# Seven half-block products for part of the output projection, a third buffer of low weight parts, and changed orders in a hybrid mLSTM / gated-MLP layer

## The chip, the core and the metric

The kernel runs on one core of a Trainium2 chip. Its engines have queues of their own: TensorE (PE, matmuls; PEld is its weight load), VectorE (DVE), ScalarE (ACT), GpSimd (POOL) and SyncE (SP), which here only issues DMAs. The metric is the device time of one execution in microseconds, the median of several runs.

## What is computed

One decoder layer over 512 tokens of width 2048: RMSNorm, one input projection (2048 to 14352 columns), two groups of heads, one output projection, residual, RMSNorm. In the reference, cut to what matters:

```python
xn = _rmsnorm(h, norm_w)
proj = jnp.einsum('bsd,de->bse', xn, w_in).astype(f32)
q, k, v_m, o_m, z_m, i_pre, f_pre, u_g, v_g, z_g = _split_cols(proj)
...
hm = _mlstm_chunkwise(q, k, v, log_i, log_f)          # 8 heads, after a causal convolution on q, k
y_m = rmsnorm(hm) * sigmoid(o_m) * silu(z_m)
...
y_g = gelu(u_g) * (W_s @ layernorm(gelu(v_g)) + b_s) * silu(z_g)
...
y = jnp.concatenate([y_m, y_g], axis=-1)
h = h + jnp.einsum('bse,ed->bsd', y, w_out)           # w_out: 4096 x 2048
return _rmsnorm(h, final_norm_w)
```

## The kernel before

All matmuls are in fp32r. For precision each operand is split into a high part (an fp32r copy, made by ACT) and a low part (the remainder, a subtraction on DVE), and each product is three matmuls: high x high, high x low, low x high.

**Stage 0** (L681 to 716) computes the first unit of the input projection in the plain way: eight steps j of 24 matmuls of 512 columns, with the gates' matmuls `gp` behind each. Beside it `split_x` and `sums_x` prepare the seven sums of blocks of x, `stats` the sums of squares, and `token_rows` (at j = 7) the row scales `r_b` with matmuls `rb_ps` from `diag` (DVE). The unit's results leave PSUM through eight Gelu activations (L713), which need `r_tok`.

**The input projection** (L719 to 748): 27 further units of 512 columns, each eight chunks of weights. A product of 2 x 2 blocks is made of seven products of sums of blocks (`PRODUCTS`, L32) in place of eight: 7 x 2 x 3 = 42 matmuls of 256 columns per chunk (L741). The seven results of a unit fill seven of the eight PSUM banks: the first four products the pool `pp`, the other three the pool `pm`, whose fourth bank serves background work. `combine` (L347) then forms the four result blocks: an ACT copy (L351) and seven DVE operations (L352 to 358). A bank is free for the next unit's product when the operation that reads it last is through; for q5 that is L356.

**Weights.** `load(n)` brings chunk n into `wf` (four buffers), four chunks ahead; a "str" chunk is five blocks of 256 columns by SP, after which POOL's DMA adds two blocks onto two others (L151). `split(n)`, two chunks ahead, forms two more sums in `we` on DVE (L175, L176), casts all seven to `wh` on ACT (L178, three buffers), and subtracts into `wl` on DVE (L179, two buffers). A "std" chunk of 1024 columns (L168, L169) serves stage 0 and the output projection.

**Background work** waits in `bg`, a queue of small steps; `run_bg(k)` runs k of them after each chunk: the activations, spatial mixing, transposes and convolution of the unit before, and in the output stage the heads of the mLSTM.

**The output projection** (L761 to 799): for the g half four column quarters dq of eight chunks, then for the mLSTM half ("m") four quarters of six chunks, all plain: 24 matmuls of 512 columns per chunk (L785 to 787), four accumulators in `pp`. While the g half runs, `gates`, `gate_columns` and the eight heads run as background, five steps a chunk: loads by POOL's queue, four score steps `st_s`, four value steps `st_sv`, `st_norm`, `st_out` (L618), and two transposes `turn` (L453) of the result `oz`, which is written to DRAM. In the last g quarter `load_y("m", g)` brings it back and splits it. The sums of the g half go through `acc_dram`.

**The last stage** (L812 to 844) adds the chunks g = 6, 7, plain, token tile by token tile, normalises and writes out.

Short-lived tiles come from a pool `tp` of 14 (tag "t"). The framework's planner, not the program text, sets the order in each engine's queue: it takes what its own model of time says is ready, earlier code first. On each engine the order is then fixed.

Of the kernel before, what the change touches and what calls it, by code (L numbers as in the profile page):

```python
# [32 lines left out]
    ("q1", 0, 1), ("q6", 4, 5), ("q2", 1, 0), ("q5", 6, 3), ("q7", 3, 4), ("q4", 2, 6), ("q3", 5, 2),  # L33
# [3 lines left out]
GAP_X, GAP_W = 32, 112  # L37
# [10 lines left out]
def hybrid_layer(ctx, tc, xs, x, w_first, w_mid, w_gate, w_out, par, bif, ws_t, sgu, fin_w, out):  # L48
# [7 lines left out]
    tp = pool("tp", 14)  # L56
# [9 lines left out]
    def temp(name, dt=F32):  # L66
        return tp.tile([P, S + 8], dt, tag="t", name=name)
# [85 lines left out]
    def split(n):  # L153
# [5 lines left out]
        if kind == "std":  # L159
# [3 lines left out]
            else:  # L163
                h, l = (wp.tile([P, WS], F32R, tag=tag, name=f"{tag}{n}", bufs=bufs)[
                    :, OFF:OFF + 1024].rearrange("p (a b) -> p a b", a=2) for tag, bufs in (("wh", 3), ("wl", 2)))
# [7 lines left out]
        l = wp.tile([P, WS], F32R, tag="wl", name=f"wl{n}", bufs=2)  # L173
        e = wp.tile([P, 2 * H], F32, tag="we", name=f"we{n}", bufs=2)
# [10 lines left out]
    def load_x(j):  # L185
        if j >= NP:
            return
        xr[j] = []
        for b in range(2):
            t = half(f"xr{j}_{b}")  # L190
# [5 lines left out]
    def split_x(j):  # L196
# [4 lines left out]
        a21 = tp.tile([P, S + 8], F32R, tag="t", name=f"a21_{j}")[:, 0:S].rearrange("p (a b) -> p a b", a=2)  # L201
# [27 lines left out]
    ssq16 = sm.tile([P, NT, 4], F32, tag="ssq16", name="ssq16", bufs=1)  # L229

    def stats(tt, half_):
        for c in (2 * half_, 2 * half_ + 1):
            t = temp(f"xt{tt}_{c}")[:, 0:S]
            nc.sync.dma_start(t, x[tt * P:(tt + 1) * P, c * S:(c + 1) * S])
            nc.scalar.activation(t, t, AF.Square, accum_out=ssq16[:, tt, c:c + 1])

    def stats_end():
        ssq = sm.tile([P, NT], F32, tag="s4", name="ssq", bufs=8)
        nc.vector.reduce_sum(ssq, ssq16, axis=mybir.AxisListType.X)
# [35 lines left out]
    def gate_spill():  # L275
        t = temp("gsp")[:, 0:S]
        nc.vector.tensor_tensor(t[0:GR, :], gp[0:GR, :], r_b[0:GR, :], op=ALU.mult)
        nc.gpsimd.dma_start(g_dram[0:GR, :], t[0:GR, :])
# [6 lines left out]
    def gates():  # L285
# [6 lines left out]
        for a, g in enumerate((li, xf)):  # L292
            nc.vector.scalar_tensor_tensor(g, in0=raw[2 + a], scalar=bif_t[:, a:a + 1], in1=g,
                                           op0=ALU.add, op1=ALU.add)
# [30 lines left out]
    def gate_columns():  # L325
        li, m, offs = gate_rows
        tps = pm.tile([P, 14, NH], F32, tag="m", name="tps")
        go = row("go")
        nn = 0
        for s0 in range(NT):  # L330
            for t0 in range(s0, NT):
# [6 lines left out]
                nc.tensor.transpose(tps[:, pair(s0, t0), :], src, ident[0:NH, 0:NH])  # L338
# [8 lines left out]
    def combine(un, q):  # L347
# [5 lines left out]
        v.tensor_tensor(a, a, ps["q2"], op=ALU.add)  # L353
        v.tensor_tensor(c, ps["q5"], b, op=ALU.subtract)
        v.tensor_tensor(d, b, ps["q7"], op=ALU.add)
# [8 lines left out]
    def st_ws(i):  # L364
        ws_s[i] = sm.tile([P, 2, P], F32, tag="ws", name=f"ws{i}")
# [122 lines left out]
    def after_qk(i, c):  # L488
        def one_tile(b, f):
# [3 lines left out]
            nc.vector.memset(q[:, 0:4], 0.0)  # L493
            for a in range(2):
                nc.vector.tensor_tensor(q[:, 4 + a * H:4 + (a + 1) * H], c[a][b][:, f, :],
                                        r_b[:, a * H:(a + 1) * H], op=ALU.mult)
            d = temp(f"qc{h}_{f}")[:, 0:S]
            nc.scalar.activation(d, q[:, 4:4 + S], AF.Identity, scale=w[:, 3:4], bias=w[:, 4:5])
            for s in (2, 1, 0):
                nc.vector.scalar_tensor_tensor(d, in0=q[:, s + 1:s + 1 + S], scalar=w[:, s:s + 1], in1=d,  # L500
# [12 lines left out]
    qk_t, v_t, cb_t, sp_t, h_t, hc_t, oz_t = {}, {}, {}, {}, {}, {}, {}  # L513
# [62 lines left out]
    def st_sv(h, t0):  # L576
        if t0 % 2 == 0:
            h_t.setdefault(h, []).append(temp(f"h{h}_{t0}")[:, 0:516].rearrange("p (a b) -> p a b", a=2))
# [338 lines left out]
```

## Time and profile before

| | us |
|---|---|
| median of 3 runs | 1608.16 (1603.77 to 1610.78) |
| profiled execution | 1603.96, span 1602.3 |
| span of stage 0, to the first product matmul | about 67 |
| input projection | about 67 to 1174 |
| output projection, g half with heads | about 1178 to 1398 |
| mLSTM half | about 1398 to 1545 with the first part of the last stage |

A row of the page's groups gives line, engine, operation, tiles, shape and count, then busy time and the mean ns of one, then the engine's idle time ahead of the group and who ended it. A row of the windows gives the stretch, its length, busy time and (instructions) for PE, PEld, DVE, ACT and POOL (for PE and PEld alone where only a line's instructions are counted), the clock granted to PE, DMA share and GB/s. A row of the waits gives who waited for whom: total us, times, longest. A row of the timeline gives start, duration, what ran, and in brackets the idle time before it. The duration of a matmul is its latency; matmuls overlap, so the distance between starts is the cost.

### The profile page before, as it was taken

Reading aid. Unit: us, or ns where it says so; the run is one execution under the profiler, and the core shown is the slowest. Engines: PE = TensorE matmul, PEld = TensorE weight load, DVE = VectorE, ACT = ScalarE, POOL = GpSimd, SP = SyncE. Lnnn points to the kernel's source line nnn. Section 1 sums busy time; section 2 is a strip of 40 time slices with the busy share of each in tenths; the row PEclk is TensorE's granted clock in tenths of the full one; section 3 lists DMA queues with packets and bytes.
Section 4 is the critical chain, followed back from the end, with each engine's and each line's share of the span. In section 5 each row is a group of like instructions: output and inputs, shape, how many; then the busy total and the mean of one; then the engine's idle time right before and its main releaser. Section 6 shows DMA issues by size and latency. Waiting matters only on the chain. (4 is left out here: it accounts for less than half of the span.)

```text
span 1602.3 us, 29051 instructions
## 1 busy us (share of the span) xinstructions
PE 1550.5 (97%) x11432; PEld 1460.3 (91%) x11432; DVE 1115.7 (70%) x1825; ACT 847.1 (53%) x1283; POOL 256.1 (16%) x360
## 2 busy tenths in 40 slices
PE   9899999999999999999999999999999999999997
PEld 8889999999999999999999999999978878788886
DVE  7787777776967876966867976669785555543354
ACT  6665455554645564554556555454685556431133
POOL 2211112211121211111211111111112121100000
PEclk9999999999999999999999999999999999999999
DMA  8768888777878787878777877887864665873332
GB/s 292 208 169 203 206 199 206 185 198 182 208 194 215 195 198 188 206 189 209 192 199 182 217 184 185 211 202 200 264 205 152 211 198 170 283 256 105 93 105 106
DMA packets 109162, 311.20 MB, mean 194 GB/s; under 512 B 12893, under 2 KB 12893, under 8 KB 109024
## 3 DMA queue, kind: packets, MB, share of 16 engines
q1 hardware_dynamic: 71568, 233.86, 47.8%
q0 software_dynamic: 36736, 74.37, 23.4%
q8 instruction: 89, 1.46, 0.4%
q10 hardware_dynamic: 720, 1.11, 0.2%
q14 instruction: 49, 0.40, 0.1%
HBM read 223.08 MB, written 29.59 MB: 158 GB/s over the span
## 5 line engine op out<-in xcount | busy, mean ns | idle before, releaser
L178 ACT CAST wh<-wf 128x1280 fp32r<-128x1280 f32 x216 | 273.2, 1265 | 348.3 <-PE q L741 271.6
L741 PE MATMUL q<-wh,xbh 128*128 128x256 f32 x1472 | 413.2, 281 | 20.4 <-DVE e L356 19.1
L179 DVE TENSOR_TENSOR wl<-wf,wh 128x1280 fp32r<-128x1280 f32 x216 | 321.5, 1488 | 131.3 <-PE q L741 128.3
L741 PE MATMUL q<-wl,xbh 128*128 128x256 f32 x1472 | 410.2, 279 | 1.1 <-DVE wl L179 0.9
L741 PE MATMUL q<-wh,xbl 128*128 128x256 f32 x1472 | 409.8, 278 | 0.0
L151 POOL DMA_DIRECT2D wf<-wf x216 | 183.7, 850 | 922.5 <-DVE wl L179 364.5
L741 PE MATMUL q<-wl,xah 128*128 128x256 f32 x1104 | 307.9, 279 | 1.5 <-DVE wl L179 1.4
L741 PE MATMUL q<-wh,xah 128*128 128x256 f32 x1104 | 309.1, 280 | 0.0
L741 PE MATMUL q<-wh,xal 128*128 128x256 f32 x1104 | 307.6, 279 | 0.0
L741 PEld LDWEIGHTS q<-wh,xbh 128*128 128x128 f32 x1472 | 278.2, 189 | 25.2 <-DVE e L356 23.5
L741 PEld LDWEIGHTS q<-wl,xbh 128*128 128x128 f32 x1472 | 277.9, 189 | 2.2 <-DVE wl L179 2.1
L741 PEld LDWEIGHTS q<-wh,xbl 128*128 128x128 f32 x1472 | 277.6, 189 | 0.0
L741 PEld LDWEIGHTS q<-wl,xah 128*128 128x128 f32 x1104 | 208.4, 189 | 2.7 <-DVE wl L179 2.4
L741 PEld LDWEIGHTS q<-wh,xah 128*128 128x128 f32 x1104 | 208.6, 189 | 0.8 <-DVE e L353 0.5
L741 PEld LDWEIGHTS q<-wh,xal 128*128 128x128 f32 x1104 | 208.1, 188 | 0.0
L175 DVE TENSOR_TENSOR we<-wf 128x256 f32<-128x256 f32 x216 | 90.7, 422 | 116.0 <-issue 77.4
L169 DVE TENSOR_TENSOR wl<-wf,wh 128x1024 fp32r<-128x1024 f32 (+1 forms) x67 | 80.9, 1207 | 117.3 <-PE om L786 52.1
L178 ACT CAST wh<-we 128x512 fp32r<-128x512 f32 x216 | 132.7, 614 | 29.4 <-DVE we L176 29.4
L179 DVE TENSOR_TENSOR wl<-we,wh 128x512 fp32r<-128x512 f32 x216 | 147.7, 684 | 0.0
L168 ACT CAST wh<-wf 128x1024 fp32r<-128x1024 f32 (+1 forms) x67 | 69.4, 1036 | 139.3 <-PE om L787 87.7
L785 PE MATMUL og<-wh,ygh 128*128 128x512 f32 x256 | 101.2, 395 | 1.1 <-DVE e L356 1.1
L787 PE MATMUL og<-wh,ygl 128*128 128x512 f32 x256 | 100.3, 392 | 0.0
(240 smaller groups left out, 2761.5 us busy)
## 6 DMA issues: line engine op xcount, KB each, us to landing
wf<-w_mid SPq DMA_DIRECT2D x216, 640.0 KB, 4.6
wf<-wf POOLq DMA_DIRECT2D x216, 256.0 KB, 5.5
wf<-w_out_p SPq DMA_DIRECT2D x64, 512.0 KB, 3.7
xr<-xs SPq DMA_DIRECT2D x16, 256.0 KB, 5.0
xt<-x SPq DMA_DIRECT2D x16, 256.0 KB, 5.6
ozd<-e SPq DMA_DIRECT2D x16, 256.0 KB, 4.2
ygd<-yfg SPq DMA_DIRECT2D x16, 256.0 KB, 4.8
vd<-e SPq DMA_DIRECT2D x16, 256.0 KB, 4.2
```

What stands on the lines that cost most here:

```text
L151: nc.gpsimd.dma_start(t[:, 3 * H:5 * H], t[:, H:3 * H], accum_op=ALU.add)
L168: nc.scalar.copy(h[:, a, :], f[:, a, :])
L169: nc.vector.tensor_tensor(l[:, a, :], f[:, a, :], h[:, a, :].bitcast(F32), op=ALU.subtract)
L175: nc.vector.tensor_tensor(e[:, 0:H], t[:, 3 * H:4 * H], t[:, 2 * H:3 * H], op=ALU.add)
L178: nc.scalar.copy(h[:, c], f)
L179: nc.vector.tensor_tensor(l[:, c], f, h[:, c].bitcast(F32), op=ALU.subtract)
L741: nc.tensor.matmul(o, lhsT=st_, rhs=mv_, start=(first and a == 0), stop=(last and a == 2), skip_group_check=True)
L785: nc.tensor.matmul(acc[q], lhsT=yh[:, kk, cs], rhs=wh[:, kk, :], start=st, stop=False)
L787: nc.tensor.matmul(acc[q], lhsT=yl[:, kk, cs], rhs=wh[:, kk, :], start=False, stop=sp_)
```

## The change

- `wl` gets three buffers, `we` one; `tp` has 12 tiles of 512 columns in place of 14 of 520, and the raw x blocks and the rows for the statistics move to `xb`.
- In `PRODUCTS` q7 stands ahead of q5, so that q5 falls to the pool `pm`; `combine` reads q7 before q5.
- 24 of the 32 mLSTM chunks (all but those of the last stage) become "str" chunks from a new packed weight `w_last`, and are computed as 42 matmuls by the function `products`, with `sums_y` forming the seven block sums of y, and `combine` at the end of each quarter. Its blocks are added to what `acc_dram` holds and go back there; the last quarter's stay in SBUF.
- `token_rows` becomes a background step behind stage 0; the gates are scaled by `r_b` later, in `gates`.
- `gate_columns` is cut in two with four pauses between; the transposes of a head move behind the next head's four score steps; six background steps a chunk in place of five in the output stage.

```diff
-    ("q1", 0, 1), ("q6", 4, 5), ("q2", 1, 0), ("q5", 6, 3), ("q7", 3, 4), ("q4", 2, 6), ("q3", 5, 2),
+    ("q1", 0, 1), ("q6", 4, 5), ("q2", 1, 0), ("q7", 3, 4), ("q5", 6, 3), ("q4", 2, 6), ("q3", 5, 2),
...
-    tp = pool("tp", 14)
+    tp = pool("tp", 12)
...
-                chunks.append(("std", w_out[int(kind == "g"), g, dq]))
+                chunks.append(("std", w_out[1, g, dq]) if kind == "g" else ("str", w_last[g, dq]))
...
-        l = wp.tile([P, WS], F32R, tag="wl", name=f"wl{n}", bufs=2)
-        e = wp.tile([P, 2 * H], F32, tag="we", name=f"we{n}", bufs=2)
+        l = wp.tile([P, WS], F32R, tag="wl", name=f"wl{n}", bufs=3)
+        e = wp.tile([P, 2 * H], F32, tag="we", name=f"we{n}", bufs=1)
...
+        raw = xb.tile([P, 4, H], F32, tag="xb", name=f"xr{j}") if j < NP - 1 else None
...
         v.tensor_tensor(a, a, ps["q2"], op=ALU.add)
+        v.tensor_tensor(d, b, ps["q7"], op=ALU.add)
         v.tensor_tensor(c, ps["q5"], b, op=ALU.subtract)
-        v.tensor_tensor(d, b, ps["q7"], op=ALU.add)
...
     def queue_head(h):
...
+        if h < NH:
+            bg.append(lambda: st_load(h))
+            bg.append(lambda: st_load_v(h))
+            bg.append(lambda: st_cb(h))
+            for s0 in range(NT):
+                bg.append(lambda s0=s0: st_s(h, s0))
+        if h > 0:
+            for f in range(2):
+                w = prm[:, C_MW + 2 * (h - 1) + f:C_MW + 2 * (h - 1) + f + 1]
+                bg.append(lambda f=f, w=w: turn("m", h - 1, f, oz_t[h - 1], w))
+            bg.append(mark(("m", h - 1)))
+        if h < NH:
+            for t0 in range(NT):
+                bg.append(lambda t0=t0: st_sv(h, t0))
+            bg.append(lambda: st_norm(h))
+            bg.append(lambda: st_out(h))
...
+    def sums_y(g):
+        ra, rb = half(f"yra{g}"), half(f"yrb{g}")
+        for f, r in enumerate((ra, rb)):
+            nc.sync.dma_start(r, y_dram[("m", g)][:, f, :].rearrange("p (a b) -> p a b", a=2))
+        ah, al = (xa.tile([P, 3, H], F32R, tag="xa", name=f"ya{c}{g}") for c in "hl")
+        bh, bl = (xb.tile([P, 4, H], F32R, tag="xb", name=f"yb{c}{g}") for c in "hl")
+        v = nc.vector
+        nc.scalar.copy(ah[:, 0, :], ra[:, 0, :])
+        nc.scalar.copy(ah[:, 1:3, :], rb)
+        v.tensor_tensor(al[:, 0, :], ra[:, 0, :], ah[:, 0, :].bitcast(F32), op=ALU.subtract)
+        v.tensor_tensor(al[:, 1:3, :], rb, ah[:, 1:3, :].bitcast(F32), op=ALU.subtract)
+        v.tensor_tensor(rb[:, 1, :], ra[:, 1, :], rb[:, 1, :], op=ALU.subtract)
+        v.tensor_tensor(ra[:, 1, :], ra[:, 0, :], ra[:, 1, :], op=ALU.subtract)
+        v.tensor_tensor(ra[:, 0, :], rb[:, 1, :], ra[:, 0, :], op=ALU.subtract)
+        v.tensor_tensor(rb[:, 0, :], rb[:, 0, :], ra[:, 0, :], op=ALU.add)
+        for b, r in enumerate((ra, rb)):
+            nc.scalar.copy(bh[:, 2 * b:2 * b + 2, :], r)
+            v.tensor_tensor(bl[:, 2 * b:2 * b + 2, :], r, bh[:, 2 * b:2 * b + 2, :].bitcast(F32), op=ALU.subtract)
...
-        if j == 7:
-            token_rows()
...
+    bg.append(token_rows)
     after_vv(0, c0)
...
     bg.append(gates)
     bg.extend([pause] * 6)
+    bg.append(gate_shifts)
+    bg.extend([pause] * 4)
     bg.append(gate_columns)
...
-        run_bg(5)
+            run_bg(6)
...
+            if g == 0:
+                q = product_banks(f"m{dq}")
+                res = {}
+                for a in range(2):
+                    for b in range(2):
+                        t = half(f"xc{dq}_{a}{b}")
+                        nc.sync.dma_start(t, block(acc_dram, a, b, dq))
+                        res[(a, b)] = t
+            products(q, Y[("m", g)], wh, wl, g == 0, g == 5, False)
+            if g == 5:
+                c = combine(f"m{dq}", q)
+                for a in range(2):
+                    for b in range(2):
+                        t = res[(a, b)]
+                        nc.vector.tensor_tensor(t, t, c[a][b], op=ALU.add)
+                        if dq < 3:
+                            nc.sync.dma_start(block(acc_dram, a, b, dq), t)
+                        else:
+                            for k in range(2):
+                                xacc[(2 * a + k, dq, b)] = t[:, k, :]
+    for tt in range(NT):
+        for dq in range(3):
+            t = row(f"xacc{tt}_{dq}")[:, 0:S]
+            nc.sync.dma_start(t, acc_dram[:, tt, dq * S:(dq + 1) * S])
+            xacc[(tt, dq)] = t
```

More of the change, by code (lines that the diff above doesn't have):

```diff
@@ L36 @@
 OFF = 16
[L37 removed]
+GAP_X, GAP_W = 24, 112
 def unit_order():
@@ L47, in hybrid_layer @@
 @with_exitstack
[L48 removed]
+def hybrid_layer(ctx, tc, xs, x, w_first, w_mid, w_gate, w_out, w_last, par, bif, ws_t, sgu, fin_w, out):
     nc = tc.nc
@@ L337, in gate_columns @@
                     nn += 1
-                nc.tensor.transpose(tps[:, pair(s0, t0), :], src, ident[0:NH, 0:NH])
+                srcs[(s0, t0)] = src
+        gate_rows.append(srcs)
+    def gate_columns():
+        li, m, offs, srcs = gate_rows
+        tps = pm.tile([P, 14, NH], F32, tag="m", name="tps")
+        for (s0, t0), src in srcs.items():
+            nc.tensor.transpose(tps[:, pair(s0, t0), :], src, ident[0:NH, 0:NH])
         for n in range(NT):
@@ L690, in hybrid_layer @@
         if 2 <= j < 6:
-            for half_ in range(2):
-                stats(j - 2, half_)
+            stats(j - 2)
         sums_x(j - 1)
@@ L715, in hybrid_layer, with product_banks, products @@
     gate_spill()
+    bg.append(token_rows)
     after_vv(0, c0)
+    def product_banks(un):
+        return {name: (pp if p < 4 else pm).tile([P, S], F32, tag="p" if p < 4 else "m", name=f"{name}_{un}")
+                for p, (name, _, _) in enumerate(PRODUCTS)}
+    def products(q, xj, wh, wl, opening, closing, features):
+        for name, xsl, wsl in PRODUCTS:
+            xh, xl = xj[xsl]
+            ps = q[name]
+            for t in range(2):
+                o = ps[:, t * H:(t + 1) * H]
+                cs = slice(t * P, (t + 1) * P)
+                first, last = opening and t == 0, closing and t == 1
+                if features:
+                    ops = ((wh[:, wsl, cs], xh), (wh[:, wsl, cs], xl), (wl[:, wsl, cs], xh))
+                else:
+                    ops = ((xh[:, cs], wh[:, wsl, :]), (xh[:, cs], wl[:, wsl, :]), (xl[:, cs], wh[:, wsl, :]))
+                for a, (st_, mv_) in enumerate(ops):
+                    nc.tensor.matmul(o, lhsT=st_, rhs=mv_, start=(first and a == 0), stop=(last and a == 2),
+                                     skip_group_check=True)
     for un in range(1, NA):
         kind, i = order[un]
-        q = {}
-        for p, (name, _, _) in enumerate(PRODUCTS):
-            q[name] = (pp if p < 4 else pm).tile([P, S], F32, tag="p" if p < 4 else "m", name=f"{name}_{un}")
+        q = product_banks(un)
         for j in range(NP):
@@ L727, in hybrid_layer @@
             split(n + 2)
-            wh, wl = splits.pop(n)
-            for name, xsl, wsl in PRODUCTS:
-                xh, xl = X[j][xsl]
-                ps = q[name]
-                for t in range(2):
-                    o = ps[:, t * H:(t + 1) * H]
-                    cs = slice(t * P, (t + 1) * P)
-                    first, last = j == 0 and t == 0, j == NP - 1 and t == 1
-                    if kind == "qk":
-                        ops = ((wh[:, wsl, cs], xh), (wh[:, wsl, cs], xl), (wl[:, wsl, cs], xh))
-                    else:
-                        ops = ((xh[:, cs], wh[:, wsl, :]), (xh[:, cs], wl[:, wsl, :]), (xl[:, cs], wh[:, wsl, :]))
-                    for a, (st_, mv_) in enumerate(ops):
-                        nc.tensor.matmul(o, lhsT=st_, rhs=mv_, start=(first and a == 0), stop=(last and a == 2),
-                                         skip_group_check=True)
+            products(q, X[j], *splits.pop(n), j == 0, j == NP - 1, kind == "qk")
             if j == NP - 1:
```

145 lines of the change are left out of this document (72 added, 73 removed).

## The prediction

> **What bounds the kernel now.** I read the page first, then the stage windows, then the waits, and last the timeline of single stops.
>
> ```profile
> span 1602.3 us, 29051 instructions
> PE 1550.5 (97%) x11432; PEld 1460.3 (91%) x11432; DVE 1115.7 (70%) x1825; ACT 847.1 (53%) x1283; POOL 256.1 (16%) x360
> ...
> 66.90:1173.50 1106.60, 1068.16 (x9069) 1054.19 (x9070) 1.00 0.79 198
> ...
> 1398.00:1545.00 147.00, 147.00 (x650) 121.76 (x649) 52.56 (x57) 37.34 (x43) 0.00 (x0) 1.00 0.47 149
> ```
>
> PE is busy nearly everywhere; DVE, second, has 30% free. The 66.9 to 1173.5 row counts only the product matmuls (L741) of the input projection; the 1398 to 1545 row is the mLSTM half of the output projection, where PE never stops. So time is won by fewer columns through PE, or by PE stops that vanish. The price of a column comes from where chunks begin in the PE timeline:
>
> ```profile
> 499.45 0.28 PE L741 MATMUL q<-wh,xah 128*128 128x256 f32 x1
> ...
> 504.21 0.28 PE L741 MATMUL q<-wh,xah 128*128 128x256 f32 x1
> ...
> 821.16 0.28 PE L741 MATMUL q<-wh,xah 128*128 128x256 f32 x1
> ...
> 826.11 0.28 PE L741 MATMUL q<-wh,xah 128*128 128x256 f32 x1
> ...
> 1420.20 0.39 PE L785 MATMUL om<-wh,ymh 128*128 128x512 f32 x1
> ...
> 1425.64 0.39 PE L785 MATMUL om<-wh,ymh 128*128 128x512 f32 x1
> ```
>
> A chunk of 42 half-width matmuls takes 4.76 us (113 ns each), sometimes 4.95 us; a chunk of 24 full-width ones takes 5.44 us (227 ns each). The cost goes with columns, with nothing per instruction. At 4.76, the 216 input chunks need 1028 us of the 1106.6; 78 us are stops, background matmuls and the slower pace. The waits name the stops:
>
> ```profile
> PE q L741 <- DVE e L356: 20.7, 18, 1.8
> PE ytm L453 <- DVE oz L618: 4.3, 5, 1.5
> PE q L741 <- DVE wl L179: 2.3, 5, 1.1
> PE ytm L453 <- issue: 2.1, 3, 1.4
> PE tps L338 <- DVE go L335: 1.5, 3, 1.1
> PE og L785 <- DVE e L356: 1.1, 1, 1.1
> ```
>
> The largest is one cause at 18 of 27 unit ends: PE wants a PSUM bank for the next unit's products that combine (L356) has not read out. One such end, DVE and PE:
>
> ```profile
> 557.09 0.42 DVE L175 TENSOR_TENSOR we<-wf 128x256 f32<-128x256 f32 x1 [1.79 <-issue]
> 557.43 0.68 DVE L352 TENSOR_TENSOR e<-e,q 128x512 f32<-128x512 f32 x1
> ...
> 559.57 0.68 DVE L355 TENSOR_TENSOR e<-e,q 128x512 f32<-128x512 f32 x1
> 560.16 1.48 DVE L179 TENSOR_TENSOR wl<-wf,wh 128x1280 fp32r<-128x1280 f32 x1
> 561.56 0.68 DVE L179 TENSOR_TENSOR wl<-we,wh 128x512 fp32r<-128x512 f32 x1
> 562.16 0.68 DVE L356 TENSOR_TENSOR e<-q,e 128x512 f32<-128x512 f32 x1
> ...
> 561.06 0.28 PE L741 MATMUL q<-wh,xal 128*128 128x256 f32 x1
> 562.90 0.38 PE L741 MATMUL q<-wh,xbh 128*128 128x256 f32 x1 [1.56 <-DVE e L356]
> ```
>
> Two L179 instructions, the low parts of a later weight chunk, stand in DVE's queue ahead of L356. They came this late because with two wl buffers they must wait until PE is through with the chunk two before, which is the unit's end.
>
> **The change part by part.** The sum is against the profiled span of 1602.3 us (1603.96 us with what lies around it); the median of the three runs is 4.2 us above that execution.
>
> A, seven products in 24 mLSTM chunks: 24 matmuls of 5.44 us become 42 of 4.76, 24 x 0.68 = **-16.3**. At the slower pace (4.95) it is -11.8; the nearest row, the same instruction on the same kind of operands, gives 4.76. The Trainium skill (TensorE: Matmul & The Clock Gate, section Back-to-back issue gap) speaks against this part: it gives about 81 ns per load-and-matmul pair at 128 columns and 131 at 512, an estimated 98 at 256, by which 42 narrow matmuls would take 4.1 us against 3.1 and the part would lose about 23 us; the 113 and 227 ns above do not agree with it.
>
> B, third wl buffer and q7 ahead of q5: with a third buffer L179 can run a whole chunk earlier, where DVE stands idle before L175 (1.79 above). The groups show that idle time:
>
> ```profile
> L175 DVE TENSOR_TENSOR we<-wf 128x256 f32<-128x256 f32 x216 | 90.7, 422 | 116.0 <-issue 77.4 <-DVE wl L179 32.2 <-DMA wf<-wf 3.3
> L179 DVE TENSOR_TENSOR wl<-wf,wh 128x1280 fp32r<-128x1280 f32 x216 | 321.5, 1488 | 131.3 <-PE q L741 128.3 <-ACT wh L178 1.0
> ...
> L169 DVE TENSOR_TENSOR wl<-wf,wh 128x1024 fp32r<-128x1024 f32 (+1 forms) x67 | 80.9, 1207 | 117.3 <-PE om L786 52.1 <-PE og L786 26.9 <-issue 24.2
> ```
>
> Without the pair L356 would start at 560.16 and end at 560.84; PE asks for the bank 0.11 after 561.06, so this stop goes wholly, even with L175 as late as now. An earlier L179 also frees wf earlier, so the load and the accumulate behind L175 start earlier. The new product order takes the fourth bank after three DVE operations; the sixth product still needs L356, but asks three matmuls (0.34 us) later. The stop above costs 1.84 - 0.11 = 1.73 where the page counts 1.56 idle, 0.17 more: 20.7 + 18 x 0.17 = 23.8. Such a stop can also drop the clock, as behind the one before 113 us:
>
> ```profile
> 113.00:117.00 4.00, 4.00 (x24) 4.00 (x23) 2.63 (x4) 3.97 (x7) 0.26 (x1) 0.61 0.78 204
> ```
>
> 4.0 x 0.39 = 1.6 us. With the 2.3 us of waits for L179 that makes 27.7 in all. I take **-25**, since some unit ends will have other DVE work in the way; the ends are -12 (half of the stops stay) and -28. One we buffer in place of two costs nothing as long as L179, in order ahead of the next L175, has read it; if ACT's cast is late it costs part of that 0.6 us, inside the same ends.
>
> C, head transposes moved behind the next head's four score steps: L618 is then done a chunk earlier.
>
> ```profile
> 1289.11 0.39 PE L785 MATMUL og<-wh,ygh 128*128 128x512 f32 x1
> 1290.95 0.33 PE L453 MATMUL ytm<-ident,oz 128*128 128x128 f32 x1 [1.45 <-DVE oz L618]
> ```
>
> 1.84 - 0.23 = 1.6 us lost here. The two ytm waits sum to 6.4 over 8 stops, 7.8 with 0.17 each. The last head has no next head and keeps its stop: **-6**, between -2 and -8.
>
> D, token_rows after the first unit:
>
> ```profile
> 53.22 0.40 PE L270 MATMUL gp<-xal,wgp 128*104 128x256 f32 x2
> 57.74 0.50 PE L248 MATMUL rb_ps<-diag,ones 128*128 128x128 f32 x2 [4.12 <-DVE diag L247]
> ...
> 58.00:67.00 9.00, 9.00 (x41) 7.50 (x41) 6.86 (x15) 5.99 (x12) 2.33 (x3) 0.81 0.45 115
> ...
> 55.88 1.48 POOL L241 TENSOR_TENSOR r_tok<-ssq,mhalf 128x4 f32<-128x4 f32 x1 [3.44 <-DVE ssq L240]
> ...
> 63.38 1.57 ACT L713 ACTIVATE e<-p,r_tok 128x256 f32<-128x256 f32 x4
> ```
>
> The stop (4.1) and the clock dip behind it (9 x 0.19 = 1.7) go, 5.8 together; the rb_ps matmuls move and still count. What is late next is the Gelu that empties the first unit's banks: it needs r_tok at 57.4, and its eight activations (0.4 each) and casts would end near 63, while unit 1 would want its fourth bank near 62. So **-4**, between 0 and -6. Statistics in 1024-column pieces and raw x in xb move work without adding any; their DMAs keep their number of bytes on SP's queue.
>
> F, gates: the transposes after six pauses wait for go (1.5), the first og matmul for L356 (1.1). Shifts four steps earlier and an earlier L356 save **-2** (0 to -3). Four tiny extra DVE operations in gates lie beside og matmuls.
>
> E, what the mLSTM chunks add elsewhere. DVE per chunk: 2 x 0.42 + 1.49 + 0.68 = 3.0 us in place of 1.2; per six chunks a combine of 7 x 0.68 and four sums of 0.68, 7.5 us, or 1.25 per chunk: 4.25 against PE's 4.76, with no background left. At a chunk with a combine DVE falls 5.8 us behind; the third buffer lends a chunk, the rest can stop PE for about 1 us, at four places, and longer if a transfer is late. The loads go from 512 to 640 KB on SP plus 256 KB accumulated by POOL, as the input stage does now:
>
> ```profile
> wf<-w_mid SPq DMA_DIRECT2D x216, 640.0 KB, 4.6
> wf<-wf POOLq DMA_DIRECT2D x216, 256.0 KB, 5.5
> wf<-w_out_p SPq DMA_DIRECT2D x64, 512.0 KB, 3.7
> ```
>
> sums_y puts 0.42 + 0.68 + 4 x 0.42 + 2 x 0.68 = 4.1 us on DVE in each of six 5.44 us chunks beside a 1.2 us split: 5.3, just fitting, and its result is wanted eight chunks later. The last quarter's two half sums add 0.15 us to the tail. **+2**, between 0 and +8.
>
> G, fewer temporaries (14 to 12) and six background steps a chunk in place of five: four of the tiles hold residual rows through a quarter, so 8 in place of 10 serve the heads, and POOL's queue waits for such tiles already:
>
> ```profile
> POOL oz L593 <- DVE vl L534: 19.5, 5, 8.8
> ```
>
> None of it reaches PE now; **+3**, between 0 and +12.
>
> Sum: -16.3 - 25 - 6 - 4 - 2 + 2 + 3 = -48.3; 1602.3 becomes 1554.0, and beside the median of 1608.16 about **1560**.
>
> **The rivals.**
>
> 1. The stops at unit ends stay: other DVE work (L175 waiting for a transfer, background steps) takes the place of the L179 pair ahead of L356, and B is only the three matmuls, 18 x 0.34 = 6. For it: the sixth product still needs L356, and L175 waits 77 us for transfers. Against: 557 to 563, where that wait did not decide. Time 1560 + 19 = 1579.
> 2. The slower pace rules: 240 chunks at 4.95 are 45 us more than at 4.76; before has part of that, at most some 15 of the 78 us above, so +30: 1590. It comes and goes at stops in the trace, and the last stage shows none of it.
> 3. Slower: temporaries. If a head's loads wait until the tiles of the head before are free, a landing (5.5 us, as POOL's accumulate), a cast and a subtract (0.7 each, as L352) and the issue stand open before L547, some 8 us per head, 64 in all: 1560 - 3 + 64 = 1621. It decides from 6 us per head. Against it: L593's waits of up to 8.8 us are hidden now, behind og matmuls.
> 4. The seven products don't save: weight loads bind narrow matmuls. The load takes 189 ns on the page:
>
> ```profile
> L741 PEld LDWEIGHTS q<-wh,xah 128*128 128x128 f32 x1104 | 208.6, 189 | 0.8 <-DVE e L353 0.5
> ```
>
> 42 x 0.189 = 7.94 against 5.44 is +60 in place of -16.3: 1636. The 4.76 us chunk consists of such pairs and refutes it; the skill's section named above belongs here.
>
> **How the numbers follow.** Forecast 0.76, around 1560, its own range 1545 to 1575. Rival 1 0.12, rival 2 0.07, rival 3 0.04, rival 4 0.01. The range runs from 1542 (A, B and C near their best ends) to 1588, which takes in rival 1. Faster by over 0.5% (below 1600; 0.5% is about what a measurement of this kernel tells from no change): 0.93. Within: 0.02, out of the first two rivals, where the worst ends of E and G meet them. Slower: 0.05, rivals 3 and 4.
>
> **What would show it.** A: chunks of the mLSTM half 4.76 apart. B: the wait of product matmuls for L356 falls from 20.7 to a few us, and L179 waits less than 128 us for PE. C: ytm's wait is left for one head. D: no rb_ps wait in front of the first unit's last chunk. E and G: new PE waits at the three quarter ends, or at the head's score and value matmuls. The prediction is wrong if product matmuls wait for another line of combine as long as for L356 now, if head matmuls wait for loads, or if the mLSTM chunks follow DVE.

## The result, and the profile after

| | before | after |
|---|---|---|
| median, 4 runs each | 1605.97 us (1598.42 to 1610.78) | 1563.81 us (1560.83 to 1567.65) |
| profiled execution | 1603.96, span 1602.3 | 1567.65, span 1565.6 |

The ratio is 0.974 (0.970 to 0.979): faster, near the forecast of 1560 and inside its range. The profiled execution of after is the longest of its four. Span against span the change is worth 36.7 us, median against median 42.2; the sum of the prediction had 48.3, and was set beside a median of 1608.16, which a fourth run of before has moved to 1605.97, so that by the same terms the forecast would now be 1557.7. The stage windows show where they differ. Each stage runs to the first matmul of the next: the first product `q`, the first `og`, the first matmul of the mLSTM half, the first `fo` of the last stage. (The bounds given for before ahead of the prediction were rough: its g half runs from 1173.88 to 1418.16 and its mLSTM half to 1548.72, so the first 20 us of the row 1398 to 1545 belong to the g half.) Columns as before: start and end, length, PE, PEld, DVE, ACT and POOL busy, granted clock, DMA share, GB/s. First before, then after:

```profile
0.00:66.89 66.89, 60.91 (x282) 51.00 (x283) 53.73 (x117) 44.24 (x95) 15.05 (x26) 0.97 0.82 262
66.89:1173.88 1106.99, 1081.32 (x9202) 1070.47 (x9201) 838.81 (x1304) 609.25 (x798) 199.04 (x235) 1.00 0.79 199
1173.88:1418.16 244.28, 233.99 (x1184) 194.78 (x1183) 148.88 (x308) 144.27 (x321) 39.83 (x95) 1.00 0.65 215
1418.16:1548.72 130.56, 130.56 (x577) 108.14 (x576) 44.36 (x46) 29.86 (x30) 0.00 (x0) 1.00 0.41 126
```

```profile
0.00:63.69 63.69, 59.12 (x275) 49.21 (x275) 51.59 (x108) 40.97 (x75) 18.46 (x21) 0.95 0.77 254
63.69:1139.99 1076.30, 1071.09 (x9208) 1066.16 (x9209) 841.09 (x1298) 613.38 (x799) 203.27 (x238) 1.00 0.79 206
1139.99:1391.08 251.09, 237.64 (x1185) 195.05 (x1184) 161.76 (x342) 154.23 (x371) 44.79 (x101) 0.99 0.63 205
1391.08:1512.13 121.05, 119.27 (x1009) 118.80 (x1008) 92.20 (x133) 48.07 (x56) 16.83 (x20) 1.00 0.92 267
```

Stage 0 is 3.2 us shorter, the input projection 30.7, the mLSTM half 9.5; the g half, which was to lose 5, is 6.8 **longer**; the last stage is 0.1 shorter. The head start of stage 0 is gone one unit later: the second unit of the stream (unit 2) starts at 106.74 before and at 106.51 after. So the balance is -0.2 to there, -33.7 for the units behind it, +6.8, -9.5, -0.1.

The waits of after, those of PE (total us, times, longest):

```profile
PE s L557 <- DVE qkl L531: 4.8, 7, 1.1
PE ytm L462 <- DVE p L569: 3.9, 4, 1.8
PE q L769 <- ACT e L745: 1.7, 2, 1.4
PE p L739 <- DVE wl L169: 1.7, 1, 1.7
PE og L821 <- ACT wh L168: 1.6, 1, 1.6
PE q L769 <- DVE wl L179: 1.6, 3, 0.9
PE p L738 <- ACT wh L168: 1.5, 1, 1.5
PE q L769 <- DVE e L362: 1.3, 1, 1.3
PE tps L349 <- ACT gb L317: 1.3, 1, 1.3
```

The 20.7 us for `combine` have become 1.3, and of those for `oz` before `ytm` 0.6 are left, at the last head. New are the first two lines: score matmuls `s` that wait for the low part `qkl` of a head's q and k, and transposes `ytm` that wait for `p` (L569, the step with which DVE empties a bank of scores). A unit end of after, on DVE; PE's first matmul of the new unit starts at 545.63, and its fourth product, 18 matmuls of some 0.113 us later, asks for the bank that L363 reads at about 547.7:

```profile
542.41 1.49 DVE L179 TENSOR_TENSOR wl<-wf,wh 128x1280 fp32r<-128x1280 f32 x1 [1.13 <-ACT wh L178]
543.82 0.68 DVE L179 TENSOR_TENSOR wl<-we,wh 128x512 fp32r<-128x512 f32 x1
544.42 0.68 DVE L361 TENSOR_TENSOR e<-e,q 128x512 f32<-128x512 f32 x1
545.02 0.42 DVE L175 TENSOR_TENSOR we<-wf 128x256 f32<-128x256 f32 x1
545.36 0.68 DVE L362 TENSOR_TENSOR e<-e,q 128x512 f32<-128x512 f32 x1
545.95 0.68 DVE L363 TENSOR_TENSOR e<-e,q 128x512 f32<-128x512 f32 x1
```

The L179 pair now stands ahead of the combine and is done before the unit ends; L175 does not wait, and L363 ends at 546.63, a microsecond early. The groups say the same of the whole run: L179 waits for ACT's cast alone, where it waited 128.3 us for PE, and L175's 77.4 us of "issue" are 14.8.

```profile
L179 DVE TENSOR_TENSOR wl<-wf,wh 128x1280 fp32r<-128x1280 f32 x240 | 356.2, 1486 | 152.8 <-ACT wh L178 152.7
...
L175 DVE TENSOR_TENSOR we<-wf 128x256 f32<-128x256 f32 x240 | 101.1, 421 | 25.8 <-issue 14.8
```

### The profile page after: what moved, and what is told of

Same layout as the page of the kernel before. It is cut to its first block, busy times and chain, and to the rows that moved or that the text cites. A ratio compares the mean times of both kernels' runs of the same rounds, so it can differ in the third digit from the quotient of the medians.

```text
span 1565.6 us, 30099 instructions
## 1 busy us (share of the span) xinstructions
PE 1531.3 (98%) x11864; PEld 1465.1 (94%) x11864; DVE 1181.9 (75%) x1944; ACT 876.7 (56%) x1340; POOL 285.6 (18%) x384
## 4 chain that ended last, share of the span: by engine, by line
PE 67%; DVE 12%; DMA 8%; issue 6%; ACT 4%; POOL 1%; SPq 0%; ACTq 0%; POOLq 0%; DVEq 0%
PE q L769 56%; DVE wl L179 2%; DMA wf<-wf 2%; PE q_m L769 1%; DMA wf<-w_mid 1%; ACT wh L178 1%; PE og L822 1%; PE og L823 1%; PE og L821 1%; DMA xr<-xs 1%; ACT jk L616 1%; PE fo L886 1%; PE fo L887 1%; PE fo L885 1%; DMA ymd<-yfm 1%
## 5 line engine op out<-in xcount | busy, mean ns | idle before, releaser
L178 ACT CAST wh<-wf 128x1280 fp32r<-128x1280 f32 x240 | 301.8, 1263 | 356.0 <-issue 205.8
L179 DVE TENSOR_TENSOR wl<-wf,wh 128x1280 fp32r<-128x1280 f32 x240 | 356.2, 1486 | 152.8 <-ACT wh L178 152.7
L151 POOL DMA_DIRECT2D wf<-wf x240 | 204.8, 855 | 997.8 <-DMA wf<-w_mid 259.6
L178 ACT CAST wh<-we 128x512 fp32r<-128x512 f32 x240 | 147.8, 616 | 94.1 <-DVE we L176 93.6
L179 DVE TENSOR_TENSOR wl<-we,wh 128x512 fp32r<-128x512 f32 x240 | 164.3, 685 | 17.2 <-ACT wh L178 17.2
L175 DVE TENSOR_TENSOR we<-wf 128x256 f32<-128x256 f32 x240 | 101.1, 421 | 25.8 <-issue 14.8
L176 DVE TENSOR_TENSOR we<-we,wf 128x256 f32<-128x256 f32 x240 | 101.1, 421 | 5.4
L822 PE MATMUL og<-wl,ygh 128*128 128x512 f32 x256 | 100.8, 394 | 0.1
```

The source lines that it names most:

```text
L151: nc.gpsimd.dma_start(t[:, 3 * H:5 * H], t[:, H:3 * H], accum_op=ALU.add)
L175: nc.vector.tensor_tensor(e[:, 0:H], t[:, 3 * H:4 * H], t[:, 2 * H:3 * H], op=ALU.add)
L176: nc.vector.tensor_tensor(e[:, H:2 * H], e[:, 0:H], t[:, 0:H], op=ALU.add)
L178: nc.scalar.copy(h[:, c], f)
L179: nc.vector.tensor_tensor(l[:, c], f, h[:, c].bitcast(F32), op=ALU.subtract)
L822: nc.tensor.matmul(acc[q], lhsT=yh[:, kk, cs], rhs=wl[:, kk, :], start=False, stop=False)
```

## The experiments

Three theories for the input projection: the third `wl` buffer took away the stops (the prediction's), the new product order did, or the single `we` buffer did, which the prediction had at nothing. For the g half: the moved transposes, the six steps, the shorter pool of temporaries, or the place of the next head's loads. Each profile was cut at the same five points. Beside the lengths stands how many of the 216 chunks of the input projection have starts that sum to 4.93 to 4.96 us, and what its length would be with each of these at 4.76 (0.187 less). That column is what PE stops and background cost, with the pace taken out; a chunk with a stop in it isn't counted, so it is good to a few us: the nine profiles with three `wl` buffers and the new order lie between 1055.6 and 1065.2.

| kernel | stage 0 | input projection | chunks at 4.95 | input at 4.76 | g half | mLSTM half |
|---|---|---|---|---|---|---|
| before | 66.9 | 1107.0 | 62 | 1095.4 | 244.3 | 130.6 |
| after | 63.7 | 1076.3 | 79 | 1061.5 | 251.1 | 121.1 |
| e1, two `wl` | 63.2 | 1086.3 | 96 | 1068.3 | 252.2 | 120.5 |
| e2, old order | 62.4 | 1085.4 | 59 | 1074.4 | 246.4 | 121.6 |
| e3, plain mLSTM half | 62.7 | 1077.4 | 65 | 1065.2 | 250.2 | 130.6 |
| e4, old transposes | 63.5 | 1082.6 | 118 | 1060.5 | 248.2 | 123.4 |
| e5, before + order | 71.4 | 1096.2 | 101 | 1077.3 | 245.0 | 130.6 |
| e6, before + one `we` | 66.3 | 1097.0 | 93 | 1079.6 | 244.2 | 130.6 |
| e7, five steps | 61.0 | 1069.3 | 48 | 1060.3 | 250.1 | 124.7 |
| e8, early loads | 62.2 | 1069.8 | 37 | 1062.9 | 241.1 | 121.6 |
| e9, `token_rows` back | 65.2 | 1086.2 | 164 | 1055.6 | 252.7 | 121.2 |
| e10, early loads + raw x | 60.3 | 1084.8 | 129 | 1060.6 | 240.0 | 123.9 |
| e11, as e8 | 62.8 | 1090.9 | 165 | 1060.0 | 242.0 | 124.2 |
| e12, as e10 | 60.4 | 1091.3 | 167 | 1060.1 | 240.0 | 121.7 |

The times of one run each: e1 to e4 on one chip 1580.17, 1570.96, 1575.69, 1574.15, beside 1607.16 of before there; e5 to e8 on another 1598.39, 1593.0, 1560.81, 1550.01, beside 1595.59; e9 1580.86, on the chip of e10 to e12. Because of the pace, and because a stage moves by some us where only the planner's order differs (stage 0 of e5 has before's code and takes 4.5 us more, with 10.2 us at a granted clock of 0.50 where before has 3.4), the stages are compared and not the times.

**e1: after with two `wl` buffers.**

```diff
-        l = wp.tile([P, WS], F32R, tag="wl", name=f"wl{n}", bufs=3)
+        l = wp.tile([P, WS], F32R, tag="wl", name=f"wl{n}", bufs=2)
```

> The changed kernel with two wl buffers again (we stays at one, the new product order stays). If the third buffer removed the stops at unit ends: PE's waits for combine come back to 15 to 25 us in all, the input projection takes 1090 to 1105 us in place of 1076, and one run takes 1578 to 1592 us. If the product order did it: waits for combine below 5 us, input projection 1070 to 1084, run at 1560 to 1568.

Waits of e1, and its group of L179:

```profile
PE q L769 <- DVE wl L179: 7.3, 8, 2.8
```

```profile
L179 DVE TENSOR_TENSOR wl<-wf,wh 128x1280 fp32r<-128x1280 f32 x240 | 357.1, 1488 | 196.1 <-PE q L769 179.6 <-PE q_m L769 14.2 <-ACT wh L178 0.9
```

DVE waits for PE again, as in before, and yet PE has no wait for `combine` left in the input projection. What comes back is that PE waits for `wl` itself, 7.3 us in place of 1.6; at the even pace the stage is 6.8 us longer than after. Neither of the two forecasts holds: the waits are those of the second, the length (1086.3) lies between the two. The third buffer is worth about 7 us here, not 25, and the stops at the unit ends go without it.

**e2: after with the old product order.**

```diff
-    ("q1", 0, 1), ("q6", 4, 5), ("q2", 1, 0), ("q7", 3, 4), ("q5", 6, 3), ("q4", 2, 6), ("q3", 5, 2),
+    ("q1", 0, 1), ("q6", 4, 5), ("q2", 1, 0), ("q5", 6, 3), ("q7", 3, 4), ("q4", 2, 6), ("q3", 5, 2),
...
-        v.tensor_tensor(d, b, ps["q7"], op=ALU.add)
         v.tensor_tensor(c, ps["q5"], b, op=ALU.subtract)
+        v.tensor_tensor(d, b, ps["q7"], op=ALU.add)
```

> The changed kernel with q5 ahead of q7 again, in the products and in combine, and three wl buffers. If the third buffer is the cause: waits of product matmuls for combine stay below 6 us and the input projection at 1070 to 1086 us (the two paces of chunks, 4.76 and 4.95, make some 8 us either way). If the order is the cause: waits of 15 to 25 us and 1090 to 1105.

```profile
PE q L769 <- DVE e L365: 5.2, 15, 1.0
```

Fifteen stops are back, a third of a microsecond each on the mean. With what follows them that is 12.9 us at the even pace: the first chunks of the 26 units behind unit 1 are together 14.9 us over 4.76, where after has 3.9. By waits and length (5.2 and 1085.4) the first forecast holds, at its upper end; but the order is worth far more than the three matmuls, 18 x 0.34 = 6, that the prediction gave it.

**e5: before with the new order alone; e6: before with one `we` buffer alone.** The edit of e5 is the diff of e2 turned round; that of e6:

```diff
-        e = wp.tile([P, 2 * H], F32, tag="we", name=f"we{n}", bufs=2)
+        e = wp.tile([P, 2 * H], F32, tag="we", name=f"we{n}", bufs=1)
```

> The kernel before with the new product order and the new order in combine alone (two wl buffers, two we buffers, 14 temporaries). If the order alone takes the stops away: PE's waits for combine fall from 20.7 to below 6 us and the input projection from 1107 to 1080 to 1092 us. If it does not, and what helped in e1 was the single we buffer: waits of 12 us or more, input projection 1095 or more.

> The kernel before with one we buffer in place of two, nothing else. If the second we buffer let L175 stand in DVE's queue ahead of combine and wait there for its transfer: L175's wait put down to issue falls from 77 us to below 20, the waits of product matmuls for combine from 20.7 to below 10, and the input projection to 1080 to 1097 us. If not: 60 us or more, 15 or more, and 1100 or more.

Waits of e5, then those of e6, its group of L175, and DVE at the end of the unit whose stop the prediction showed:

```profile
PE q L741 <- DVE e L356: 11.9, 11, 1.6
```

```profile
PE q L741 <- DVE wl L179: 7.5, 12, 2.4
PE q L741 <- DVE e L356: 4.9, 4, 2.0
```

```profile
L175 DVE TENSOR_TENSOR we<-wf 128x256 f32<-128x256 f32 x216 | 91.2, 422 | 5.9 <-DMA wf<-wf 1.7
```

```profile
555.00 0.42 DVE L175 TENSOR_TENSOR we<-wf 128x256 f32<-128x256 f32 x1
...
557.47 1.49 DVE L179 TENSOR_TENSOR wl<-wf,wh 128x1280 fp32r<-128x1280 f32 x1
558.87 0.68 DVE L179 TENSOR_TENSOR wl<-we,wh 128x512 fp32r<-128x512 f32 x1
559.47 0.69 DVE L356 TENSOR_TENSOR e<-q,e 128x512 f32<-128x512 f32 x1
```

The order alone takes the combine's wait from 20.7 to 11.9 (the input projection takes 1096.2: the second forecast, but for 0.1 us of wait). The single buffer alone takes it to 4.9, and all three figures of its first forecast hold: with one `we` the planner places L175 behind the L179 that reads `we` before, later in DVE's order, and its 77.4 us of standing first in line for a transfer, with the combine queued behind, are gone. That "issue" was a transfer: 40 of these 42 waits in before's trace end 0.08 or 0.09 us after one of POOL's accumulates into `wf` has landed.

The unit end shows which wait counted. In e6 the unit starts at 557.19; the L179 pair still stands right ahead of L356, as in before, but L175 found its transfer landed and stands behind the first step of combine. L356 is through 2.97 us after the unit's start, in before 4.84, and the longest distance between PE's starts in that chunk falls from 1.84 to 0.18 us. So the pair that the prediction named need not leave its place: the 1.79 us of L175 ahead of combine were enough to make the stop. The price is 7.5 us of waits for `wl`, the ones that e1 has too and that the third buffer removes. At the even pace: order alone -18, one `we` alone -16, both with two `wl` -27 (e1), with three -34. What the third buffer does alone, with two `we` and the old order, which is the prediction's own mechanism, was not tried: it is not needed for most of the gain, and whether it would have been enough stays open.

**e3: after with the mLSTM half plain.** The products, the combine and the block sums of y are replaced by the plain matmuls; the result is the same.

```diff
-                chunks.append(("std", w_out[1, g, dq]) if kind == "g" else ("str", w_last[g, dq]))
+                chunks.append(("std", w_out[int(kind == "g"), g, dq]))
...
-            products(q, Y[("m", g)], wh, wl, g == 0, g == 5, False)
```

> The changed kernel with the 24 mLSTM chunks plain, 24 matmuls of 512 columns each, and without the block sums of y. If the cost goes with columns: the mLSTM half takes 130.6 us (24 x 5.44), or 135.7 if the slower pace falls on it, against 121.05 in the changed kernel's profile, and its first 1.4 us wait goes. If the block sums of y or the larger chunks burden the g half, that falls by 3 us or more from 251; if not, it stays within 3 us.

The window of its mLSTM half:

```profile
1390.22:1520.78 130.56, 130.56 (x578) 108.19 (x576) 45.45 (x47) 31.17 (x32) 0.00 (x0) 1.00 0.38 122
```

130.56 us, to the hundredth what before has, and a g half of 250.2, both as forecast for a cost that goes with columns. So the products are worth 9.5 in their own stage, and `sums_y` costs the g half nothing that can be seen.

**e4: the transposes at their old place; e7: five steps a chunk.**

```diff
-        if h > 0:
-            for f in range(2):
-                w = prm[:, C_MW + 2 * (h - 1) + f:C_MW + 2 * (h - 1) + f + 1]
-                bg.append(lambda f=f, w=w: turn("m", h - 1, f, oz_t[h - 1], w))
-            bg.append(mark(("m", h - 1)))
...
         bg.append(lambda: st_out(h))
+        for f in range(2):
+            w = prm[:, C_MW + 2 * h + f:C_MW + 2 * h + f + 1]
+            bg.append(lambda f=f, w=w: turn("m", h, f, oz_t[h], w))
+        bg.append(mark(("m", h)))
```

```diff
-            run_bg(6)
+            run_bg(5)
```

> The changed kernel with the two transposes of a head right behind st_out again, six steps a chunk. If the new waits of the score matmuls for the low part of q and k (5.5 us over 10 waits) come from the moved transposes, because the next head's loads and subtractions now stand right behind the normalisation chain that holds DVE: these waits fall below 1 us, transposes wait 4 to 8 us again, and the g half takes 244 to 251 us. If six steps a chunk or 12 temporaries are the cause: score matmuls still wait 4 us or more, the transposes' waits come on top, and the g half takes 253 us or more.

> The changed kernel with five background steps a chunk in the output stage in place of six. If six steps squeeze the heads: the score matmuls' waits for the low part of q and k fall from 5.5 to below 2 us and the g half from 251 to 244 to 248 us. If the place of the loads behind the normalisation chain is the cause: these waits stay at 4 us or more and the g half at 249 to 253.

Waits of e4, then of e7:

```profile
PE ytm L462 <- DVE oz L628: 10.1, 8, 1.5
```

```profile
PE ytm L462 <- DVE oz L628: 5.2, 1, 5.2
...
PE s L557 <- DVE qkl L531: 3.2, 5, 0.8
...
PE ytm L462 <- DVE p L569: 2.3, 3, 1.3
```

With the old place the waits for `qkl` and for `p` (9.4 us in after) vanish and eight stops before `ytm` take their place (10.1, more than the 4 to 8 forecast): 248.2 against 251.1 for the stage. The stop was not removed by the move; it was handed on. With five steps the waits for `qkl` and `p` fall from 9.4 to 6.2 us, but the last head ends later and its transposes wait 5.2 us; the stage stays at 250.1. So six steps are not what lengthens the stage, though they add to the waits between heads.

**e8: after, with the next head's loads queued ahead of `st_norm`.**

```diff
+    def queue_load(h):
+        if h < NH:
+            bg.append(lambda: st_load(h))
+            bg.append(lambda: st_load_v(h))
+            bg.append(lambda: st_cb(h))
+
     def queue_head(h):
-        if h < NH:
-            bg.append(lambda: st_load(h))
-            bg.append(lambda: st_load_v(h))
-            bg.append(lambda: st_cb(h))
+        if h == 0:
+            queue_load(0)
...
+            queue_load(h + 1)
             bg.append(lambda: st_norm(h))
             bg.append(lambda: st_out(h))
```

The reason for it lies in after's timeline, at the head that starts at 1233, ACT, DVE, POOL and PE together:

```profile
1231.44 1.12 ACT L530 CAST qkh<-qr 128x512 fp32r<-128x512 f32 x2
...
1231.57 0.17 DVE L618 TENSOR_SCALAR sq<-sq 128x4 f32<-128x4 f32 x1 [2.64 <-ACT jk L616]
...
1232.40 1.04 POOL L620 TENSOR_TENSOR rn<-sq,mhalf 128x4 f32<-128x4 f32 x1
...
1233.47 0.16 DVE L622 TENSOR_TENSOR hc<-rr,rn 128x4 f32<-128x4 f32 x1 [1.73 <-POOL rn L620]
1233.55 0.69 DVE L531 TENSOR_TENSOR qkl<-qr,qkh 128x512 fp32r<-128x512 f32 x1
...
1234.30 0.50 PE L557 MATMUL s<-qkl,qkh 128*128 128x512 f32 x1 [0.76 <-DVE qkl L531]
```

ACT's cast of the new head is through at 1232.56, and DVE is free. But L531 stands in DVE's queue behind `hc` of the head before, whose chain runs over ACT (`jk`), DVE, POOL (`rn`) and back. DVE waits 2.64 and 1.73 us at the head of that chain, L531 starts 1.0 us late, and PE stops for it.

> The changed kernel with the loads of the next head (st_load, st_load_v, st_cb) queued ahead of st_norm in place of behind st_out. If DVE, held by the normalisation chain ahead of the subtractions of q and k, is the cause: the score matmuls' waits fall below 1.5 us, the transposes' stay below 4, and the g half takes 243 to 248 us in place of 251. If loads wait for temporaries instead: score matmuls still wait 3 us or more, or wait on the cast or the load, and the g half stays at 249 or more.

The g half of e8, as a window:

```profile
1132.06:1373.18 241.12, 235.84 (x1185) 197.18 (x1183) 160.54 (x340) 151.03 (x369) 44.65 (x101) 0.99 0.64 211
```

No score matmul waits any more, and `p` no longer holds `ytm`. PE stands still for 241.12 - 235.84 = 5.3 us in place of 13.5, and the stage is 10 us shorter than after's and 3.2 shorter than before's. e10, e11 and e12 have the same edit and 240.0 to 242.0; the seven profiles of after's kind without it have 246.4 to 252.7. That settles the cause: the queue place of the loads. The forecast of 243 to 248 was too cautious.

**e9: `token_rows` back in stage 0.**

```diff
+        if j == 7:
+            token_rows()
...
-    bg.append(token_rows)
```

> The changed kernel with token_rows at step 7 of stage 0 again. If its move is worth the 4 us of the prediction: a wait of PE for diag of 3 us or more and a clock dip return, and the second of the units made of seven products (the third unit) begins 2 to 6 us later than the 102.3 to 106.5 us of the kernels that have it moved, that is at 106 to 110 us. If what is late next (the Gelu that empties the banks, the moved matmuls) takes all of it: it begins within 102 to 106 us.

The first product matmul and the first of the second chunk, in PE's timeline of e9, then of after:

```profile
65.24 0.28 PE L769 MATMUL q<-wh,xah 128*128 128x256 f32 x1
...
70.18 0.28 PE L769 MATMUL q<-wh,xah 128*128 128x256 f32 x1
```

```profile
63.69 0.38 PE L769 MATMUL q<-wh,xah 128*128 128x256 f32 x1 [0.26 <-ACT e L745]
...
70.75 0.36 PE L769 MATMUL q<-wh,xah 128*128 128x256 f32 x1
```

After is 1.6 us ahead at the start of the stream and 0.6 behind one chunk later: its first chunk takes 7.06 us, with the wait of 1.4 us for the Gelu activations (`ACT e`) that could begin only when `r_tok` was there. e9 has no such wait and reaches unit 2 at 104.81, after at 106.51, the other profiles with after's start between 102.33 and 105.39. The wait for `diag` that returns is 1.8 us, not 3. `token_rows` behind stage 0 is worth nothing that these runs can tell.

**e10: e8, and the raw x of step 0 in two tiles, as in before. e11: e8 once more, in four runs. e12: e10 once more, in six runs.**

```diff
-        raw = xb.tile([P, 4, H], F32, tag="xb", name=f"xr{j}") if j < NP - 1 else None
+        raw = xb.tile([P, 4, H], F32, tag="xb", name=f"xr{j}") if 0 < j < NP - 1 else None
```

> Early loads of the next head (as in e8), and the raw x of step 0 in two tiles of the temporary pool again, as in the kernel before, so that the first loads stand as they did there. If the start is slow because the one tile for both halves changed the order of the first loads and subtractions: the two waits of the first matmuls (1.3 to 1.7 us each) go, the clock is full some 3 us earlier, stage 0 takes 59 to 61 us, and the ratio to before is 0.962 to 0.970. If not: stage 0 stays at 61 to 64 and the ratio is that of e8's kernel.

> The kernel of e8, timed. If the 10 us that its g half was shorter than the changed kernel's hold: ratio to before 0.964 to 0.972, against 0.974 of the changed kernel. If e8's run was a lucky draw of paces: 0.972 to 0.978.

> The kernel of e10 once more, with five rounds. If the pace of chunks, 4.76 or 4.95, is drawn anew by each session on a chip and sets the spread: the profile's stage 0 (59 to 62) and g half (239 to 243) come out as in e10, while the input projection lies anywhere from 1068 to 1092 us with 30 to 170 slow chunks, and the ratio to before in 0.960 to 0.980. If the ratio of 0.977 was the kernel itself: input projection within 3 us of 1084.8, ratio within 0.974 to 0.980.

The start, 5 to 10 and 10 to 15 us, of after and then of e10:

```profile
5.00:10.00 5.00, 1.81 (x7) 1.12 (x6) 2.70 (x6) 2.37 (x5) 1.02 (x3) 0.83 0.96 360
10.00:15.00 5.00, 5.00 (x13) 3.89 (x13) 5.00 (x13) 3.29 (x8) 3.11 (x2) 0.50 1.04 398
```

```profile
5.00:10.00 5.00, 4.09 (x11) 2.90 (x11) 3.60 (x8) 2.00 (x5) 0.86 (x3) 1.00 1.00 371
10.00:15.00 5.00, 5.00 (x25) 4.08 (x23) 5.00 (x13) 3.61 (x8) 1.82 (x2) 1.00 1.04 398
```

After's PE stands for 3.2 of the five microseconds from 5 to 10 and then runs five more at a granted clock of 0.50, 13 matmuls where e10 has 25. With both halves of the first raw x in one tile the first loads and DVE operations come in another order, and the low part of the first weights is ready later (L169 starts at 8.81 in after, at 5.67 in e10). Stage 0 is 60.3 and 60.4 us in e10 and e12, 61.0 to 63.7 in the profiles of after's start. Part of that range is not the edit: after, e1, e4 and e11 have 6.8 us at a granted clock of 0.50 there (62.8 to 63.7), e2, e3, e7 and e8, with the same code for this stage, none (61.0 to 62.7).

The times, all on one chip: e10 1564.22 (4 runs), ratio 0.977 (0.971 to 0.983); e11 1571.03 (4 runs), 0.981 (0.976 to 0.986); e12 1569.71 (6 runs), 0.980 (0.977 to 0.984). The forecasts of these ratios for e10 and e11 were missed, those of the stages of e10 and e12 held; e12's input projection, 1091.3 with 167 slow chunks, is 6.6 us longer than e10's, so e10's 1084.8 was not the kernel itself. By its stages, at one pace, e10 should beat after by some 12 us (stage 0 by 3.4, the input projection by 1, the g half by 11, less 3 in the mLSTM half); these ratios don't show it, since after was not timed on that chip, and the pace (below) differs by more than that. The nearest comparison in time is among the profiles of that chip with equal numbers of slow chunks: e9, after but for one step, has a span of 1578.8 us (164 of them), e11 1573.4 (165), e12 1566.9 (167), one execution each. That the kernel of e10 and e12 is the better one is read from its stages; no timed comparison with after shows it.

## Why the prediction was right, and where it was not

**B, right in direction, too small, and put down to one edit of three, which was not needed for most of it.** -25 was forecast; the units behind unit 1 lost 33.7. The sum counted idle time, and one clock dip of 1.6 us. In PE's timeline of before the first chunks of the 27 units are 34.6 us over 4.76: 26.0 in distances between starts of over 0.3 us, 6.0 in distances of 0.19 to 0.3, and the rest is the slower pace. Of the 6.0, 2.6 are in the two units where the granted clock fell to 0.50 (the row 113 to 117, and once more at 976); the other 3.4 are mostly single distances of 0.22 in place of 0.113 behind the stops, which no wait counts. Behind unit 1 all of it is 3.9 in after. The steps that failed are "One we buffer in place of two costs nothing" and the 0.34 us for the order: alone, either of them wins about half of it (e5, e6), and the third buffer pays for the `wl` waits that they bring (e1, e2). The mechanism was right as far as the queue goes: work that isn't ready stood in DVE's queue ahead of the combine. But L175 counted as well as L179, the row with 77.4 us of "issue" that the prediction quoted and set aside ("557 to 563, where that wait did not decide"); e6 takes the stop away at that very unit end with the L179 pair in its place.

**A, right per chunk, at the other pace; E, right at that pace only.** Chunk starts in after's mLSTM half are 4.95 us apart, in 21 of 24 chunks:

```profile
1412.22 0.28 PE L769 MATMUL q_m<-wh,yah 128*128 128x256 f32 x1
...
1417.17 0.28 PE L769 MATMUL q_m<-wh,yah 128*128 128x256 f32 x1
```

That is the prediction's other value: 24 x (5.44 - 4.95) = 11.8, less 2.3 of stops, 9.5. But the pace was not the whole of it. In e9 20 of the 24 chunks take 4.76 and the half is as long, 121.2: the first chunks of three quarters and the last chunk of all take 5.99, 6.37, 6.10 and 7.51, together 6.9 us over. At the quicker pace combine and the sums behind it come later than PE wants them (2.6 us for the ACT copy of combine at the last stage's first matmul). The half took 120.5 to 124.7 in all ten profiles that have the products, at either pace. So A and E together are worth 6 to 10, not 14; in after the pace takes 4.5 of it (11.8 for 16.3), and where the pace is quick the term "+2" is too small. The Trainium skill (TensorE: Matmul & The Clock Gate, section Back-to-back issue gap), by which an estimated 98 ns a pair would have made this part lose, does not agree with these chunks either: 4.95 / 42 is 118 ns.

**C and G, wrong in sign: +6.8 for C, F and G in place of -5.** The step that failed is C, "L618 is then done a chunk earlier". It is, and the transposes wait for `oz` only 0.6 us, but 3.9 for `p`, where before had 7.0 in all. And PE now comes to the next head's score steps while DVE still does the normalisation, and what is late next is L531 (5.5 us). The prediction asked for that at the mLSTM chunks and at the loads, not in DVE's queue at this place; its test "if head matmuls wait for loads" names the symptom. Of the 6.8, 3.2 are idle time (13.5 against 10.3) and 3.6 longer busy time of the same matmuls; 3.4 us at a granted clock of 0.50, at 1216.6 behind a stop of 1.8, are an estimated 1.7 of these, half of their length. Of G, six steps in place of five make 1.0 us of difference to the stage (e7). The 12 temporaries were not tried by themselves; with early loads the stage is below before's in spite of them. Why e4, with the old place, has 10.1 us of `ytm` waits and before only 7.0 stays open.

**F, nothing in place of -2.** Before had 1.5 for `tps` and 1.1 for the first `og`; after has 1.3 and 1.6, at the same two places with other releasers.

**D, nothing in place of -4**, the upper end of its range. The stop and the dip went, 3.2 us by the start of the stream; the Gelu that the prediction named as late next took it back, and a slower start took its share, an edit (the raw x in `xb`) that the prediction had as moving work "without adding any".

So the total came out 12 us short of its terms, and that it lies so near the forecast is luck: two errors partly met, B was 9 us better than its term, and C, F, G, D, A and E together some 20 worse. Rival 1 (the stops stay) fell with 1.3 us of combine waits; rival 3's place was right, head matmuls that wait for loads, but not its cause or its 8 us per head; rival 4 fell as above. Rival 2 (the slower pace) is half true, and is taken up below.

## What to carry to other kernels

When an engine with an ordered queue makes another wait, list everything that stands ahead of the late instruction, and ask of each what it waits for itself; a smaller buffer can help there, because it makes the planner place the waiting work later. A stop that is moved away from one consumer goes to the next thing that shares the queue: put loads for the next round ahead of the long chain of this round, not behind it. And compare stages, not whole times, when a part of the time moves between runs for a reason that the change does not touch.

## What was not expected of the hardware

**Two paces of the same matmuls.** Back-to-back products run at 4.76 or at 4.95 us per chunk of 42, with hardly anything between, and the granted clock is 1.00 in both. e8 and e11 are one and the same kernel; the input projection of the first, then of the second:

```profile
62.24:1132.06 1069.82, 1065.25 (x9210) 1059.86 (x9209) 841.89 (x1296) 613.25 (x798) 203.15 (x238) 1.00 0.79 207
```

```profile
62.76:1153.65 1090.89, 1086.93 (x9210) 1082.41 (x9209) 841.47 (x1298) 612.81 (x799) 203.73 (x238) 1.00 0.78 203
```

The same 9210 matmuls are busy for 21.7 us more, while PE is idle for 4.6 and 4.0. 37 chunks take 4.95 in e8, 165 in e11, and 128 x 0.187 = 23.9. A chunk's pace is that of the one before it unless the stream breaks between them (a stop, or other matmuls), with one exception that stands out in the traces: behind each of the four units of kind `qk`, in which the weight block is the operand `lhsT` and the x block `rhs`, the other way round than in the next unit. In the ten profiles without a stop at these places the input projection's pace changes at 36 of these 40 places, in either direction, and at one other place of their unbroken streams. The profiles of e9 to e12, on one chip, have 129 to 167 such chunks, those of e7 and e8, on another, 48 and 37, while e5 and e6 on the chip of e7 and e8 have 101 and 93. The plain chunks of the mLSTM half show 5.44, all 24 of them, in each of the four profiles that have them. What sets the pace was not found: no experiment changed it on purpose, and e12 shows only that one kernel can have 129 or 167 slow chunks on one chip. Rival 2's 1590 assumed it for the whole kernel, and the measured effect of most chunks at 4.95 is about that size: some 25 us.

**The granted clock halves behind some stops of under 2 us, and not behind others like them.** In before's input projection it is 0.50 for 3.41 us twice, at 112.7 and 976.3, 0.3 and 1.1 us behind stops of 1.82 and 1.81 us; four other stops there of 1.76 to 1.81 us have no such stretch. What decides was not found. Nor is a slow start always in that record: e8, with after's code for stage 0, has 16 matmuls in its window 10 to 15, at a granted clock of 1.00, where e10 has 25. With these stretches, and with the 0.22 us distances behind stops in before, the idle time that a waits table adds up is a lower bound of what a stop costs.
